# Matrices of group B beside the heads of group A, inverses on two engines beside the gates, and TensorE's order in the scan written by hand

## The chip, the cores and the metric

The kernel is one program on one core of a Trainium2 chip. The metric is its device time in microseconds (us). Engines: TensorE (PE in the profile; PEld is its weight load), VectorE (DVE), ScalarE (ACT), GpSimd (POOL) and SyncE (SP), whose one queue issues all of this kernel's DMA in order.

## The reference

One layer of a bidirectional recurrence backbone for 2048 latent and 128 context tokens, model width 1024: two head groups that read one input projection, an output projection, then a SwiGLU. Cut to what the change touches:

```python
def hgrn2_scan(q, k, v, g, s0):            # group A: 4 heads, two directions
    G = jnp.cumsum(g, axis=-2)
    q_dec, k_dec = q * jnp.exp(G), k * jnp.exp(-G)
    attn = jnp.where(causal, einsum(q_dec, k_dec), 0.0)
    ...                                     # S_t = diag(exp g_t) S_{t-1} + k_t v_t^T

def gated_delta_scan(q, k, v, beta, g, s0): # group B: 4 heads, two directions
    k_beta = k * beta[..., None]
    lower = jnp.where(strict, einsum(k_beta, k) * decay_mask, 0.0)
    sol = triangular_solve(lower + eye, concat([v * beta, k_beta * exp(G)]))
    u, w = sol[..., :dv], sol[..., dv:]
    attn = einsum(q, k) * decay_mask
    def step(s, inp):                       # one chunk after the other
        v_new = u_c - einsum(w_c, s)
        o_c = einsum(q_c, s) + einsum(attn_c, v_new)
        s = s * d_c + einsum(kt_c, v_new)

y = concat([o_a, o_b]) @ w_out              # after per-head norm and gate
x = x + g1 * y                              # then norm, SwiGLU, residual, final norm
```

## The kernel before, in words

Tokens are cut into 17 chunks of 128 (16 latent, one context, c = 16). Projections run as float32r triples (high by high, low by high, high by low part), in 5 pieces of 3 or 4 chunks. A plain float32 matmul has two records in the profile. The stages, in the order of the program:

- **Input norm and the convolved q, k, v of group B**, left in DRAM (`qkv_d`).
- **Heads of group A** (`for h in range(H)`): per head four projections and the chunked recurrence in both directions. Their matmuls write `pj`, `pa`, `pk`, `pu`, `po`.
- **The gate stage** (`sG`): eight gate projections (`gate_block`), and beside them the inverses of group B's triangular matrices, in three parts. `A1` makes a chunk's two matrices: k by k on PE into `pkk`, decays by a masked Exp, eight products on DVE, a sum on POOL, and a store. `A2` inverts all 32 x 32 diagonal blocks of a batch of chunks at once, in a chain of 60 dependent element-wise operations on one engine (tiles `pr`, `A`). `A3` puts a chunk's inverse together from the blocks by two levels of small matmuls (`pl`, `pn`), and stores it. There are five batches: four of four latent chunks, and the context chunk. `A2` runs on DVE for three batches and on POOL for two. `A1` has one buffer for the keys (`kTa`).
- **The scan of group B**, 16 iterations `i`: one chunk forward (c = i) and one backward (c = 15 - i). A scan step of one direction is six groups of four matmuls, `pkS`, `pv`, `pS`, `po`, `pa`, and `pqk` of the chunk that comes next. Between them lie the hops of the recurrence: `pkS`, then DVE makes `vn` (four operations, L929), `pv`, then ACT copies `vv` (L935), `pS`, then DVE makes the new state (L943). **Output steps** run beside it: `out_a` (norm, four transposes `ot`, gate, split in high and low), `out_b` (24 matmuls `py`, residual), `out_c` (norm and transposes `nt`, for five chunks). There are 34, one for each chunk and head group: the 17 of group A (part 0) can run at any time, the 17 of group B (part 1) only when both directions have passed the chunk, which for latent chunks is from i = 8 on. `first` and `todo` hold them. Before the loop eight part-0 steps are issued; the rest are spread so that part 0 is through by i = 7.
- **The SwiGLU** (`z`, `y`), in three sweeps.

Which instruction follows which on an engine is decided when the program is built, by the program's order, the priorities in it and a scheduler; each engine then runs its list in order. `tc.high_priority` moves a block ahead; `tc.issue_after` keeps a block behind an instruction.

Of the kernel before, what the change touches and what calls it, by code (L numbers as in the profile page):

```python
# [33 lines left out]
def hybrid_step(ctx: ExitStack, tc, x, vecs, ada1, ada2, bada, win, wgt, alog, dtb, sa, sb, wout, wg, wu, wd, normf,  # L34
# [106 lines left out]
    gq = pool(sK, "gq", right=True)  # L141
# [298 lines left out]

    with ExitStack() as sA:
        ap_ = pool(sA, "ap", 1)
        smask = ap_.tile([P, 512], F32, tag="smask", name="smask")
# [12 lines left out]
        for h in range(H):  # L456
# [3 lines left out]
            for i, (c0, n) in enumerate(PIECES):  # L460
# [4 lines left out]
                                               op1=ALU.mult)  # L465
            w = load_w(win[12 + h])
            for i, (c0, n) in enumerate(PIECES):
# [6 lines left out]
                nc.scalar.activation(out=vt[i], in_=pt[:, :n], func=AF.Copy, scale=0.5)  # L474
            for d in range(2):
# [7 lines left out]
                for i in order:  # L483
# [79 lines left out]
                    dma(out=oav[:, c0:c0 + n, h, :], in_=og)  # L563

    sp1.close()

    def bcast_G(t, d, c):
        dma(out=t.rearrange("p h t -> p (h t)"),
            in_=gr_d[d].rearrange("(c h) t -> c (h t)", h=H)[c:c + 1, :].broadcast_to([P, H * P]))
# [6 lines left out]
    psl = pool(s1b, "psl", 2, PSUM)  # L576
    psp = pool(s1b, "psp", 2, PSUM)


    with ExitStack() as sG:  # L580
        gp = pool(sG, "gp", right=True)
# [3 lines left out]

        def A1(c, b, j):

            kT = W([P, H, P], "kTa")
            dma(out=kT, in_=qkv_d[c, :, 0])
            pk = psp.tile([P, H, P], F32, tag="pre", name="pkk")  # L590
            for h in range(H):
                nc.tensor.matmul(out=pk[:, h], lhsT=kT[:, h], rhs=kT[:, h], start=True, stop=True)
            es = []
            for d in range(2):
                e = W([P, H, P], "e", 4)
                es.append(e)
                bcast_G(e, d, c)
                s = 1 if d == 0 else -1
                nc.gpsimd.affine_select(out=e, in_=e, pattern=[[0, H], [-s, P]], compare_op=ALU.is_gt, fill=1e30,
                                        base=0, channel_multiplier=s)  # L600
                for h in range(H):
                    nc.scalar.activation(out=e[:, h], in_=e[:, h], func=AF.Exp, scale=-1.0, bias=G[:, d, c, h:h + 1])
                for h in range(H):
                    nc.vector.scalar_tensor_tensor(out=e[:, h], in0=pk[:, h], scalar=nrho[:, d, c, h:h + 1],
                                                   in1=e[:, h], op0=ALU.mult, op1=ALU.mult)
            nc.gpsimd.tensor_tensor(out=es[0], in0=es[0], in1=es[1], op=ALU.add)
            dma(out=tri(b, j, [[P, P], [4 * BQ, H], [1, P]]), in_=es[0])

        def A2_load(b):
# [5 lines left out]
            B = W([P, 32, 32], "B")  # L615
# [10 lines left out]
        def A2(b, A, e=nc.vector):  # L626
# [4 lines left out]
            pr = W([P, 240], "pr")  # L631
# [6 lines left out]
            T = W([P, 32, 32], "B")  # L638
# [6 lines left out]
        XT = [W([P, 2, H, P], f"XT{i}") for i in range(2)]  # L645
        NS = [W([P, 2, H, 64], "NS")]
# [3 lines left out]
        def A3(c, b, j):  # L650
# [3 lines left out]
            xt = XT[n % 2]  # L654
            second = n >= NB[1] and n % 2 == 1

            dd = W([P, 2, 2, H, 32], "e", 4) if second else W([P, 2, 2, H, 32], "dd", 2)
            dma(out=dd.rearrange("p a d h s -> p (a d h) s"),
                in_=xi_d[b][j].rearrange("a d (h q) (i s) -> (q i) (a d h) s", q=4, s=32))
            L = W([P, H, P], "e", 4) if second else W([P, H, P], "L", 2)  # L660
            dma(out=L, in_=tri(b, j, [[P, P], [4 * BQ, H], [1, P]]))
            if second and len(NS) < 2:
                NS.append(W([P, 2, H, 64], "kTa"))
                nc.gpsimd.memset(NS[1], 0.0)
            na, s6 = (NS[int(second)][:, i] for i in range(2))
# [894 lines left out]
```

## Time and profile before

| | |
|---|---|
| median of 3 runs | 3353.89 us (3351.26 to 3354.86) |
| the profiled execution: time, span | 3358.57 us, 3356.9 us |
| PE busy, mean granted clock | 3121.5 us (93%), 0.964 of full speed |
| DVE, ACT, POOL busy | 2089.0, 1519.0, 1254.8 us |
| DMA, mean | 185 GB/s |

A busy PE is not a PE at its peak: a matmul's record is longer than its turn in a stream of them, and at half clock all of it takes twice as long. So stages are compared by the windows below, and matmuls are priced from the distance between the starts of two that follow each other closely.

### The profile page before, as it was taken

The numbers are of one execution on the slowest core, as the hardware profiler recorded it, in microseconds if no ns is written. First come the engines' busy times: TensorE is split into PE (matmuls) and PEld (weight loads), VectorE is DVE, ScalarE is ACT, GpSimd is POOL, SyncE is SP. The second block draws the span as 40 slices with busy tenths as digits, with TensorE's granted clock in tenths as the row PEclk, the third lists the DMA queues.
The fourth block names the chain that finished last, engine by engine and source line by source line (L and its number), as shares of the span: only waits on it lengthen the run. The fifth ranks groups of instructions, "written<-read, shape, count | busy, mean of one in ns | idle before, by whom it ended". The sixth has DMA issues, their size and how long they took to land. (4 is left out here: it accounts for less than half of the span.)

```text
span 3356.9 us, 51604 instructions
## 1 busy us (share of the span) xinstructions
PE 3121.5 (93%) x18550; PEld 2792.2 (83%) x18550; DVE 2089.0 (62%) x4016; ACT 1519.0 (45%) x3233; POOL 1254.8 (37%) x1228
## 2 busy tenths in 40 slices
PE   7899989999999799998897999999999999899998
PEld 4687779999998677877786888888899998799997
DVE  4667744474553764564666777778565677565667
ACT  6455435374464544663764555454422223422222
POOL 1100001021121337413566544554545553544446
PEclk8999999999999988999998999999999999999999
DMA  5235410111114667877784877898656766655564
GB/s 221 72 109 145 116 55 29 53 44 36 53 39 138 172 179 230 265 249 253 240 263 152 304 287 286 298 325 314 223 192 212 240 211 230 228 193 194 184 201 155
DMA packets 331009, 620.12 MB, mean 185 GB/s; under 512 B 77818, under 2 KB 177954, under 8 KB 324354
## 3 DMA queue, kind: packets, MB, share of 16 engines
q1 hardware_dynamic: 330754, 616.83, 56.0%
q8 instruction: 147, 2.41, 0.3%
q14 instruction: 108, 0.88, 0.1%
HBM read 435.22 MB, written 181.51 MB: 184 GB/s over the span
## 5 line engine op out<-in xcount | busy, mean ns | idle before, releaser
L257 PE MATMUL pj<-hh,wh 128*128 128x384 f32 (+2 forms) x1480 | 546.0, 369 | 12.9 <-DVE q L464 6.6
L257 PE MATMUL pj<-hl,wh 128*128 128x384 f32 (+2 forms) x1480 | 545.2, 368 | 0.3 <-POOL hl L231 0.3
L257 PE MATMUL pj<-hh,wl 128*128 128x384 f32 (+2 forms) x1480 | 545.3, 369 | 0.0
L257 PEld LDWEIGHTS pj<-hh,wh 128*128 128x128 f32 (+1 forms) x1480 | 280.4, 189 | 45.5 <-DVE q L464 6.8
L257 PEld LDWEIGHTS pj<-hl,wh 128*128 128x128 f32 (+1 forms) x1480 | 280.1, 189 | 29.9 <-issue 3.1
L257 PEld LDWEIGHTS pj<-hh,wl 128*128 128x128 f32 (+1 forms) x1480 | 280.1, 189 | 28.7 <-issue 3.3
L1476 POOL TENSOR_TENSOR u<-u,g 128x384 f32<-128x384 f32 (+1 forms) x132 | 136.3, 1033 | 292.7 <-DVE u L1217 242.8
L494 POOL TENSOR_SCALAR th<-th,nlbh,lbh 128x384 f32<-128x384 f32 (+1 forms) x40 | 60.5, 1513 | 405.8 <-ACT G L492 401.8
L1371 DVE TENSOR_TENSOR acc<-y,acc 128x512 f32<-128x512 f32 x192 | 131.7, 688 | 64.9 <-PE y L1367 58.0
L1209 PE MATMUL z<-x1h,wp 128*128 128x384 f32 (+1 forms) x528 | 142.8, 334 | 17.6 <-ACT wp L1067 14.2
L1067 ACT ACTIVATE wd<-wdr 128x512 fp32r<-128x512 f32 x146 | 90.0, 627 | 149.4 <-PE y L1367 95.4
L1367 PE MATMUL y<-wd,hid0h 128*128 128x512 f32 x432 | 136.4, 399 | 18.7 <-ACT hid0h L1067 10.0
L1464 ACT ACTIVATE g<-g 128x384 f32<-128x384 f32 (+1 forms) x132 | 66.7, 505 | 191.0 <-DVE g L1217 190.1
L1067 ACT ACTIVATE hid0h<-u 128x384 fp32r<-128x384 f32 (+3 forms) x113 | 53.3, 481 | 217.2 <-POOL u L1476 181.2
L1209 PE MATMUL z<-x6h,wp 128*128 128x384 f32 (+1 forms) x528 | 142.7, 333 | 7.2 <-ACT wp L1067 4.6
L246 DVE TENSOR_TENSOR wl<-raw,wh 128x512 fp32r<-128x512 f32 (+1 forms) x74 | 51.7, 698 | 153.6 <-ACT wh L245 153.5
L1371 DVE TENSOR_TENSOR sum<-y,sum 128x512 f32<-128x512 f32 x144 | 99.3, 690 | 75.8 <-PE y L1367 73.3
L1209 PE MATMUL z<-x4h,wp 128*128 128x384 f32 (+1 forms) x528 | 144.5, 331 | 1.3 <-DMA wp<-wpd 1.3
L1209 PE MATMUL z<-x7h,wp 128*128 128x384 f32 (+1 forms) x528 | 144.3, 332 | 1.0 <-DMA wp<-wpd 1.0
L1068 DVE TENSOR_TENSOR wd<-wdr,wd 128x512 fp32r<-128x512 f32 x146 | 111.9, 775 | 51.5 <-ACT wd L1067 50.6
L1209 PE MATMUL z<-x3h,wp 128*128 128x384 f32 (+1 forms) x528 | 142.6, 328 | 0.0
L1209 PE MATMUL z<-x2h,wp 128*128 128x384 f32 (+1 forms) x528 | 140.5, 328 | 1.4 <-DMA wp<-wpd 1.4
(414 smaller groups left out, 8850.6 us busy)
## 6 DMA issues: line engine op xcount, KB each, us to landing
wp<-wpd SPq DMA_DIRECT2D x308, 512.0 KB
wpd<-wp SPq DMA_DIRECT2D x154, 512.0 KB
ld<-qkvd SPq DMA_DIRECT2D x34, 1024.0 KB
wdr<-in_wd_dram SPq DMA_DIRECT2D x66, 512.0 KB
raw<-in_win_dram SPq DMA_DIRECT2D x72, 256.0 KB
e<-grd SPq DMA_DIRECT2D x68, 256.0 KB
at<-in_ada_dram SPq DMA_DIRECT2D x64, 256.0 KB
wr<-in_wg_dram SPq DMA_DIRECT2D x22, 512.0 KB
```

Of the source, the lines that this page charges most:

```text
L246: nc.vector.tensor_tensor(out=wl[:, ks], in0=raw, in1=wh[:, ks], op=ALU.subtract)
L257: nc.tensor.matmul(out=out, lhsT=a[:, k], rhs=b[:, k], start=t == 0, stop=t == 3 * KD - 1)
L494: nc.gpsimd.tensor_scalar(out=th, in0=th, scalar1=nlbh[:, col:col + 1], scalar2=lbh[:, col:col + 1], op0=ALU.mult, op1=ALU.add)
L1067: nc.scalar.activation(out=wh, in_=raw, func=AF.Copy)
L1068: (e or nc.vector).tensor_tensor(out=wl, in0=raw, in1=wh, op=ALU.subtract)
L1209: nc.tensor.matmul(out=z, lhsT=w_[:, k], rhs=x_[:, k, :N], start=t == 0, stop=t == 3 * HK - 1)
L1367: nc.tensor.matmul(out=py, lhsT=u_[:, j * P:j * P + P], rhs=v_, start=t == 0, stop=t == 2)
L1371: nc.vector.tensor_tensor(out=sums[i, j], in0=py, in1=sums[i, j], op=ALU.add)
L1464: nc.scalar.activation(out=g, in_=g, func=AF.Silu)
L1476: nc.gpsimd.tensor_tensor(out=us[i], in0=us[i], in1=gs[i], op=ALU.mult)
```

## The change

Three things are moved.

1. **Matrices beside the heads.** `A1` leaves the gate stage. Loads, decays and products of the 17 chunks are issued in small steps after the pieces of group A's projections (`beside`), with two buffers, in the space of a gate tile that is now given back earlier. Its `pkk` uses the PSUM tag `tr`, with two banks that `pk` and `ptv` of the heads use too.
2. **Inverses in two chains.** All `A2` are issued at the head of the gate stage, on DVE for batches 1, 2, 0 and on POOL for 3 and 4; then all `A3`, with three result tiles, two scratch tiles and four PSUM banks, then the gates.
3. **The scan's order on PE.** Inside `tc.manual_schedule(engines={PE})` PE keeps the order of the program. A scan step is a generator that yields after each group of matmuls; an output step is a list of pieces (three `py` matmuls, or four transposes), and the pieces are dealt out between the groups. An iteration takes two output steps throughout; the four parts of an output step lie in successive steps. Other engines are still ordered by the scheduler.

```diff
+        def A1(c, b, j, kT, es):
+            pk = ps1.tile([P, H, P], F32, tag="tr", name="pkk", bufs=2)
+            for h in range(H):
+                nc.tensor.matmul(out=pk[:, h], lhsT=kT[:, h], rhs=kT[:, h], start=True, stop=True)
...
+        chunk = [lambda: A1_decays(*held[0]), matrices]
+        steps = [load_next] * 2 + chunk * len(loads)
+        slots = [0, 5 * 4 * H]
+        def beside():
+            slots[0] += 1
+            while steps and len(steps) * (slots[1] - 8) > (slots[1] - 4 - slots[0]) * nsteps:
+                steps.pop(0)()
...
-        for t in range(5):
-            for j, c in enumerate(batches[order[t]]):
-                A1(c, order[t], j)
-            blocks.append(A2_load(order[t]))
-            if t:
-                chain(t - 1)
-            if t == 1:
-                levels(0)
-        chain(4)
-        for t in range(1, 5):
-            levels(t)
+        for b in (1, 3, 2, 4, 0):
+            with tc.high_priority(1000):
+                A2(b, A2_load(b), nc.gpsimd if b in (3, 4) else nc.vector)
+        for b in border:
+            for j, c in enumerate(batches[b]):
+                A3(c, b, j)
         for b in range(8):
             gate_block(b)
...
+    with tc.manual_schedule(engines={mybir.EngineType.PE}):
+        for _ in range(2):
+            for f in out_step():
+                f()
...
+        for i in range(NL):
+            cs = (i, NL - 1 - i)
+            gens = [scan(d, cs[d], pres[d]) for d in range(2)]
+            nxt = [scan_load(0, i + 1), scan_load(1, NL - 2 - i)] if i < NL - 1 else None
+            groups_ = [lambda g=g: next(g, None) for _ in range(5) for g in gens]
+            if nxt:
+                for d in range(2):
+                    groups_.append(lambda d=d: scan_pq(*nxt[d]))
...
+            for j, g in enumerate(groups_):
+                if j in (0, len(groups_) // 2):
+                    for f in fill:
+                        f()
+                    fill = out_step()
+                    left = len(groups_) // 2 if j == 0 else len(groups_) - j
...
+                g()
+                for _ in range(-(-len(fill) // left)):
+                    fill.pop(0)()
+                left -= 1
```

On PE, at the end of the gate stage (`pj` is a gate projection, `pl` and `pn` are `A3`, `ot` to `pv` the first output and scan steps). Before:

```order
L257 MATMUL pj<-hh_600,wl 128x384
L681 MATMUL pl_10216<-kTa,e 32x32 x16
...
L686 MATMUL pn_10332<-dd,NS 32x32 x4
L701 MATMUL pl_10347<-NS 64x64 x8
L675 MATMUL pl_10380<-e 32x32 x16
L820 MATMUL ot<-ident,o_12304 128x128
L905 MATMUL pqk<-ld 128x128 x4
L927 MATMUL pkS<-S_12783,ld 128x128
...
L681 MATMUL pl_10380<-kTa,e 32x32 x16
L686 MATMUL pn_10414<-e,kTa 32x32 x4
L933 MATMUL pv<-ld,XT 128x128 x4
```

In the change, the end of the last `A3` and what follows it:

```order
L736 MATMUL pl_10928<-XT_9256,L 64x64 x4
L726 MATMUL pn_10913<-dd,NS_9260 32x32 x4
L715 MATMUL pl_10961<-dd,L 32x32 x9
L741 MATMUL pl_10928<-NS_9260 64x64 x8
L721 MATMUL pl_10961<-NS_9259,dd 32x32 x16
L726 MATMUL pn_10995<-dd,NS_9259 32x32 x4
L736 MATMUL pl_11010<-XT_9257,L 64x64 x8
L726 MATMUL pn_10995<-dd,NS_9259 32x32 x4
L741 MATMUL pl_11010<-NS_9259 64x64 x8
L941 MATMUL pqk<-ld 128x128 x8
L961 MATMUL pkS<-S_12311,ld 128x128 x4
L880 MATMUL py<-woh,oh 128x512
```

Before, the last eight chunks of `A3` (of 17) stood between matmuls of the scan and of output steps, the very last after 240 `py`. Now nine chunks stand among the gates, the first after 267 matmuls of the gate projections that follow the last `po` of the heads, and eight stand alone after the last gate matmul, ahead of every scan matmul.

On PE in the scan, in an iteration past the middle, the first groups of both directions. Before (one direction; 20 `py` stand between `pkS` and `pv`, 16 of them left out here):

```order
L905 MATMUL pqk<-ld 128x128 x4
L847 MATMUL py<-woh,oh 128x512
L847 MATMUL py<-wol,oh 128x512
L847 MATMUL py<-woh,oh 128x512
L847 MATMUL py<-wol,oh 128x512
L927 MATMUL pkS<-S_15500,ld 128x128 x4
L847 MATMUL py<-woh,ol 128x512
...
L933 MATMUL pv<-ld,XT 128x128 x4
L947 MATMUL po<-S_15500,ld 128x128 x4
L820 MATMUL ot<-ident,ob 128x128 x4
L938 MATMUL pS<-vv,ld 128x128 x4
L954 MATMUL pa<-vv,e 128x128 x4
```

In the change:

```order
L961 MATMUL pkS<-S_15119,ld 128x128 x4
L906 MATMUL nt<-ident,xn 128x128 x4
...
L961 MATMUL pkS<-S_15132,ld 128x128 x4
...
L968 MATMUL pv<-ld,XT 128x128 x4
L849 MATMUL ot<-ident,ob 128x128 x4
L906 MATMUL nt<-ident,xn 128x128 x4
L968 MATMUL pv<-ld,XT 128x128 x4
...
L974 MATMUL pS<-vv,ld 128x128 x4
L880 MATMUL py<-woh,oh 128x512
...
L974 MATMUL pS<-vv,ld 128x128 x4
```

The two directions now run side by side, a half iteration's output step is dealt out in threes and sixes between their groups, and `po` and `pa` come behind both `pS`. The order of the SwiGLU's matmuls, from the first `z` on, and all matmuls ahead of the first `pkk` are the same in both programs.

## Rows read from the trace of the kernel before

**Rows 1.** Windows by stage: engine busy us (records), granted PE clock, DMA share, GB/s.
```profile
490.00:1038.00 548.00, 535.04 (x3247) 499.80 (x3248) 286.50 (x694) 279.97 (x439) 98.80 (x82) 0.99 0.14 43
1038.00:1298.00 260.00, 226.69 (x1805) 201.14 (x1805) 144.49 (x395) 126.82 (x256) 98.64 (x157) 0.93 0.64 175
1298.00:1316.00 18.00, 11.53 (x220) 10.60 (x214) 11.95 (x34) 14.32 (x44) 9.95 (x25) 0.58 0.89 265
1316.00:1525.00 209.00, 199.94 (x1801) 171.62 (x1799) 122.57 (x319) 129.64 (x388) 74.71 (x119) 0.95 0.80 263
1525.00:1610.00 85.00, 68.61 (x498) 64.70 (x497) 39.48 (x114) 34.97 (x99) 29.93 (x32) 0.93 0.75 255
1610.00:1803.00 193.00, 176.11 (x1061) 153.75 (x1061) 126.97 (x333) 123.17 (x348) 113.89 (x99) 0.94 0.72 231
1803.00:1835.00 32.00, 26.09 (x107) 19.33 (x105) 20.28 (x34) 11.12 (x37) 21.06 (x16) 0.84 0.48 164
1835.00:1848.00 13.00, 0.06 (x1) 0.00 (x0) 12.85 (x11) 5.65 (x12) 11.31 (x8) 0.71 0.37 120
1848.00:3357.00 1509.00, 1443.64 (x7722) 1334.56 (x7722) 1016.02 (x1677) 542.47 (x1039) 764.28 (x650) 0.98 0.69 238
```
**Rows 2.** PE groups, 1038 to 1316: count, busy us, mean ns, idle before and releaser.
```profile
L592 PE MATMUL pkk<-kTa 128*128 128x128 f32 x136 | 21.2, 305 | 30.8 <-DMA kTa<-qkvd 30.1 <-DVE pr L635 0.6
```
**Rows 3.** PE groups, 490 to 1038.
```profile
L521 PE MATMUL pk<-ident,e 128*128 128x128 f32 x136 | 26.9, 275 | 8.3 <-DVE e L516 8.3
```
**Rows 4.** PE timeline in the scan at full clock: start us, us, what.
```profile
1508.22 0.39 PE L847 MATMUL py<-woh,oh 128*128 128x512 f32 x1
...
1510.53 0.40 PE L847 MATMUL py<-wol,oh 128*128 128x512 f32 x1
...
1552.64 1.06 PE L954 MATMUL pa<-vv,e 128*128 128x128 f32 x8
1553.53 1.06 PE L905 MATMUL pqk<-ld 128*128 128x128 f32 x8
```
**Rows 5.** PE timeline, 1298 to 1316: small matmuls of A3 nearly alone.
```profile
1300.24 0.93 PE L696 MATMUL pl<-XT,e 64*64 64x64 f32 x16 [0.19 <-DVE XT L690]
...
1305.09 0.60 PE L686 MATMUL pn<-dd,NS 32*32 32x32 f32 x8
1308.85 1.57 PE L696 MATMUL pl<-XT,L 64*64 64x64 f32 x16 [3.16 <-DVE XT L690]
...
1313.38 1.57 PE L701 MATMUL pl<-NS 64*64 64x64 f32 x16 [2.40 <-ACT NS L698]
1314.88 1.35 PE L675 MATMUL pl<-e 32*32 32x32 f32 x32
```
**Rows 6.** Line L635 of A2: durations ns min/median/max, first and last start.
```profile
L635 DVE TENSOR_TENSOR pr<-A x90: 190/366/1373, 1095.8 to 1245.8; 128x30 f32<-128x30 f32 x6, 128x58 f32<-128x58 f32 x6, 128x84 f32<-128x84 f32 x6, 128x108 f32<-128x108 f32 x6
L635 POOL TENSOR_TENSOR pr<-A x60: 231/534/1376, 1246.3 to 1376.0; 128x30 f32<-128x30 f32 x2, 128x58 f32<-128x58 f32 x2, 128x84 f32<-128x84 f32 x2, 128x108 f32<-128x108 f32 x2
```
**Rows 7.** POOL groups, 1037 to 1320.
```profile
L606 POOL TENSOR_TENSOR e<-e 128x512 f32<-128x512 f32 x17 | 23.4, 1379 | 20.4 <-DVE e L604 16.9 <-DVE A L637 3.3
```
**Rows 8.** PE groups, 1316 to 1848.
```profile
L847 PE MATMUL py<-woh,oh 128*128 128x512 f32 x272 | 113.5, 417 | 4.6 <-ACT oh L822 4.0 <-DVE xt L855 0.5
...
L938 PE MATMUL pS<-vv,ld 128*128 128x128 f32 x272 | 42.7, 306 | 12.5 <-ACT vv L935 11.6 <-POOL A L637 0.8
```
**Rows 9.** PE groups, 1610 to 1803.
```profile
L927 PE MATMUL pkS<-S,ld 128*128 128x128 f32 x112 | 14.8, 275 | 0.0
```
**Rows 10.** Who PE waited for, 1316 to 1848: us in total, times, longest.
```profile
PE pS L938 <- ACT vv L935: 11.6, 13, 2.9
```
**Rows 11.** DVE, ACT and POOL groups, 1465 to 1835.
```profile
L929 DVE SCALAR_TENSOR_TENSOR ld<-pkS,nrg,ld 128x128 f32<-128x128 f32 x100 | 28.1, 342 | 8.8 <-PE pkS L927 7.0 <-DMA x<-in_x_dram 1.1
...
L935 ACT ACTIVATE vv<-pv 128x512 f32<-128x512 f32 x28 | 16.4, 584 | 23.5 <-PE pv L933 23.5
...
L908 POOL TENSOR_TENSOR ld<-ld,vbs 128x512 f32<-128x512 f32 x23 | 25.0, 1086 | 104.9 <-DMA ld<-qkvd 75.5 <-DVE ol L823 13.5 <-PE po L947 5.8
```

More of the change, by code (lines that the diff above doesn't have):

```diff
@@ L563, in hybrid_step @@
                     dma(out=oav[:, c0:c0 + n, h, :], in_=og)
+                    beside()
+        assert not steps
     sp1.close()
-    def bcast_G(t, d, c):
-        dma(out=t.rearrange("p h t -> p (h t)"),
-            in_=gr_d[d].rearrange("(c h) t -> c (h t)", h=H)[c:c + 1, :].broadcast_to([P, H * P]))
     def rep_h(m):
@@ L584, in W @@
             return gp.tile(shape, dt, tag=tag, name=tag, bufs=bufs)
[L586 to L607, printed above, removed]
         def A2_load(b):
@@ L909, in scan_pre, with scan_pq @@
                                     .to_broadcast([P, H, P]), op=ALU.mult)
+    def scan_pq(kT, qT, kn, vn, e, X):
+        pq = ps2.tile([P, H, P], F32, tag="pre", name="pqk", bufs=1)
+        for h in range(H):
+            nc.tensor.matmul(out=pq[:, h], lhsT=kT[:, h], rhs=qT[:, h], start=True, stop=True)
+        nc.vector.tensor_tensor(out=e, in0=pq, in1=e, op=ALU.mult)
     visited = set()
-    last = [None]
+    todo = []
     def scan(d, c, pre):
@@ L951, in scan @@
             dma(out=o_sb[d].rearrange("h k v -> k h v"), in_=Sn)
-        pa = sc_("pa")
-        for h in range(H):
-            last[0] = nc.tensor.matmul(out=pa[:, h], lhsT=at[:, h], rhs=vv[:, h], start=True, stop=True)
         second = c in visited
@@ L963, in scan @@
                 nc.scalar.activation(out=t[:, h], in_=po[:, h], func=AF.Copy, scale=eG[:, d, c, h:h + 1])
+        yield
+        pa = sc_("pa")
+        for h in range(H):
+            nc.tensor.matmul(out=pa[:, h], lhsT=at[:, h], rhs=vv[:, h], start=True, stop=True)
+        if lat:
             nc.vector.tensor_tensor(out=t, in0=pa, in1=t, op=ALU.add)
@@ L990, in scan_ctx @@
-    def scan_ctx():
-        ts = []
-        for d in range(2):
-            a = scan_load(d, NL)
-            scan_pre(d, NL, *a)
-            ts.append(scan(d, NL, a))
-            visited.discard(NL)
-        nc.gpsimd.tensor_tensor(out=ts[0], in0=ts[0], in1=ts[1], op=ALU.add)
-        return ts[0]
+        if not lat:
+            ctx_o.append(t)
+            if d:
+                nc.gpsimd.tensor_tensor(out=ctx_o[0], in0=ctx_o[0], in1=ctx_o[1], op=ALU.add)
+                todo.append((NL, 1, ctx_o[0]))
+            else:
+                visited.discard(NL)
+        elif not second:
+            dma(out=ob_d[c], in_=t)
+        else:
+            of = W([P, H, P], "or", 2)
+            dma(out=of, in_=ob_d[c])
+            nc.gpsimd.tensor_tensor(out=t, in0=t, in1=of, op=ALU.add)
+            todo.append((c, 1, t))
@@ L1002, in hybrid_step @@
     first = [(c, 0, None) for c in halves[0] + halves[1]]
-    todo = []
-    for _ in range(8):
-        out_step(first.pop(0))
     for d in range(2):
```

271 lines of the change are left out of this document (156 added, 115 removed).

## The prediction

> **What bounds the kernel now.** I read the page first, then windows cut at the stages. In the heads PE is busy 535.0 of 548 us at a granted clock of 0.99, and in the SwiGLU 1443.6 of 1509 us at 0.98: PE sets the time there, and the change leaves the SwiGLU's order alone [rows 1]. What can be won lies between 1038 and 1848 us. In the gate stage (1038 to 1298) PE is busy 226.7 of 260 us, and its groups say why: `pkk` waited 30.8 us, nearly all for the keys' DMA into a single buffer [rows 1, 2]. From 1298 to 1316 only the small matmuls of `A3` are there, and PE is at a clock of 0.58. Then comes the scan, 1316 to 1835, 519 us.
>
> To see how far the scan is from what its matmuls need, I price them by distance of starts at full clock. From the `py` at 1508.22 to the tenth after it at 1510.53 is 2.31 us, so 0.231 us each; a group of four float32 matmuls (eight records) follows the one before in 0.89 us, 0.111 a record [rows 4]. The scan has 816 `py` (three lines of 272) and six groups of 256 or 272 records each, 1600 in all [rows 8], and about 176 transposes at a record's price each: 188 + 178 + 20 = 386 us. Eight of the 17 chunks of `A3` lie in there too, by the order of the program. A chunk's small matmuls take 0.60 + 1.57 + 1.57 + two times 1.35 = 6.4 us at about half clock [rows 5], so some 3.2 at full clock, 26 us for eight. So PE needs 412 of the 519 us, 79%. The stretches differ. From 1525 to 1610 no output step is left that can run, the recurrence runs alone, and PE is busy 68.6 of 85 us. From 1610 to 1803, 14 steps of a direction (112 `pkS` records, eight a step) run with an output step beside each [rows 1, 9]. One costs six times 0.89, plus 24 times 0.231, plus 0.45 for transposes, 11.3 us; 14 make 159 of 193 us, 82%.
>
> No other engine is full: in that stretch DVE is busy 127 us, ACT 123, POOL 114 [rows 1], per iteration (two directions, 27.6 us) 18.1, 17.6 and 16.3 us. DMA moves 231 to 263 GB/s from 1316 to 1803, at a share of 0.72 to 0.80.
>
> **The change, part by part.**
>
> *Heads.* 17 chunks of `A1` add 136 records at 0.111, 15 us, on an engine that is full. Their work on ACT, DVE and POOL lies beside: these are busy 280, 287 and 99 of 548 us [rows 1]. `pkk` shares two PSUM banks with the transposes `pk`, which already wait 8.3 us for DVE in this stage [rows 3], so I add 2: **+17 us**. Bounds: 15 with no new wait; 50 if each of the 17 waits the 2 us that those four (one a head) do.
>
> *Gates.* From 1038 to 1316 are 278 us, with the gates, `A1` and nine chunks of `A3`. Out go the waits before `pkk`, 31, and its matmuls, 15; the 18 us alone at the end become a chunk and a half among gate matmuls, say 6 us, so 12 less [rows 1, 2]. The clock of 0.93 means that 14% of the stage ran at half speed, mostly where PE waited; I take 4 us back. That leaves 216 us. The first inverse is needed after 267 gate matmuls. The gates' own share is 216 less nine chunks at 3.2, 187 us, for 960 matmuls, 0.195 each: 52 us after the heads. A DVE chain alone is 60 operations at a median 0.366, a POOL chain 60 at 0.534 [rows 6], so 22 and 32 us, and with loads, a transposition and the splits of weights DVE's is ready well before. But the two have not yet run together: DVE's three end at 1246, POOL's begin at 1246.3 [rows 6]. The nearest sign of what they do to each other is that the longest DVE operation of the chain took 1373 ns, as long as POOL's sum of two matrices (mean 1379) that ran in the same stage [rows 6, 7]. If each operation waits out the other's, a pair takes 0.90 us and both chains 54; with some 8 us of loads ahead the first matmul of `A3` would stand on PE for 10 us, and all gate matmuls behind it. I take **6**, between 0 and 20. The stage: 222 for 278, **-56 us**.
>
> The Trainium skill, "SBUF — State Buffer", section "Who interferes with whom", says that a VectorE instruction with two SBUF inputs contends with a GpSimd instruction that reads SBUF. The trace's 1373 ns agrees; by that rule alone the term would be 10, not 6.
>
> *`A3` alone.* Eight chunks now stand behind the last gate matmul with nothing else for PE. Bounds: the matmuls at half clock, 6.4 us, or less where two chunks overlap and the clock holds (3.2); and the distance of two chunks at this same level now, 1300.24 to 1308.85, 8.6 us [rows 5]. ACT is shared with the first output steps as it is there, but there are three result tiles and four banks where there were two. I take 6: **+48 us**, between 26 and 69. The same eight leave the scan, which is counted next.
>
> *Scan.* An iteration is two steps of a direction and two output steps, 22.6 us by price. The hops: `vn` is four DVE operations of 342 ns, 1.4 us, `vv` one copy of 0.58 [rows 11]; between a `pkS` and its `pv` now lie six or nine `py`, the other direction's `pkS` and transposes, about 3.4 us, so that hop is covered unless its engine is late, and likewise `pv` to `pS` (2.5 us or more). The stretch without output steps is gone. In the first half I take PE at 86%: better than the 82% of 1610 to 1803, since part 0 has neither residual nor POOL work. With 45 `py` an iteration (the last four steps fall behind the loop) and 7 us for the context chunk that is 181 / 0.86 = 211. In the second half an iteration also moves, by the tiles in the code, two of each: `ld` 1024 KB, `XT`, `e`, `or`, `gt` 256 KB, `xt`, `x2` and its store 512 KB, in all 7.3 MB. At 82% PE gives 212 for eight; at 263 GB/s, the rate of the fullest long stretch [rows 1], the loads give 28 each, 223. I take 218. Behind the loop some 99 `py` at 0.231, 23 us, and waits, 32; ahead of it 4. The sum is 465 for 519, **-54 us**. Bounds: 386 / 0.92 = 420; and 386 / 0.76 = 508, below the worst long stretch.
>
> *Boundary to the SwiGLU.* 13 us with PE idle [rows 1]; its first weights are still loaded when the scan's tiles come free, so 0.
>
> Sum: 17 - 56 + 48 - 54 = -45 us. The profiled execution took 3358.6 (span 3356.9, the rest around it), which gives 3314; the median of the runs shown is 4.7 lower than that, so **3309**.
>
> **The rivals.**
>
> *A, the forecast:* about -45 (3285 to 3335).
>
> *B, the order covers all.* PE in the scan gets near its 96% busy of 1316 to 1525 without its half-clock stretches: 386 / 0.92 = 420 and `A3` at 4.5 a chunk: -45 - 45 - 12, some 3250. For it: the hops are covered two times over, and no engine is over 70% of an iteration. Against: two thirds of ACT, DVE and POOL each, in strict lists, make some operation late in every iteration.
>
> *C, the loads set the second half.* POOL already waits 75.5 us for `ld` in 1465 to 1835 [rows 11]. At 231 GB/s, the rate of 1610 to 1803, an iteration takes 32 us: +36 us, 3345. Against: that rate was not a limit, the share was 0.72.
>
> *D, the written order stalls, slower.* Today the scheduler may put `pqk`, `po` and 20 `py` wherever it found room; now a late hop stops everything behind it. The mechanism: `vv` waits in ACT's list behind eight Exps and eight squares of the output steps. PE waited 13 times for `vv`, at most 2.9 us [rows 10]. With four such hops an iteration (`vv` and the state, both directions), 64 in all, it is slower than before from 45 / 64 = 0.7 us a hop beyond my 82 to 86%; at 1.5 us each it would be +51, 3405.
>
> *E, a wash.* The tail of `A3` at 8.6 a chunk (+21) and the chains' wait at 20 (+14) leave -10: 3344.
>
> The bound of a change that can be told from none is about 0.2%, 7 us.
>
> **How the numbers follow.** A 0.42, B 0.20, C 0.15, D 0.14, E 0.09. Faster by over 0.2%: A, B, most of C and half of E, 0.78. Same: the rest of those two, 0.07. Slower: D and a little, 0.15. The range leaves out the lower part of B and D: 3245 to 3352. The likeliest case alone has 3285 to 3335.
>
> **What would show it.** Heads: longer by 15 to 20 us, `pkk` without waits over a few us in all. Gates: no wait for `kTa`; a wait of PE at the first `pl` for `XT` or `dd`, and longer medians in both chains, would show the two engines in each other's way. `A3` alone: a stretch of about 48 us with PE half idle and at a low clock, between the last `pj` and the first `pqk`. Scan: `pkS` of one direction every 26 us in the first half and 27 in the second, no stretch without `py`, clock above 0.97. Waits of PE at `pS` for `vv` far above 12 us would speak for D; PE waiting at `pv` or `pkS` for DMA, and a DMA share above 0.85, for C. I am wrong if the tail of `A3` is much longer than 48 us, or if the scan stays above 500.

## The result: 0.9% slower

The changed kernel took a median 3384.8 us (3383.2 to 3387.3), before 3354.4 beside it: ratio 1.0093, 95% interval 1.0076 to 1.0111. Forecast were 3309 and, at 0.78, a gain. The profiled execution has a span of 3384.2 for 3356.9, so 27.3 us are to be found. First windows by stage of the changed kernel, columns as in [rows 1]:

```profile
488.00:1074.00 586.00, 555.13 (x3376) 513.53 (x3376) 328.82 (x830) 316.26 (x572) 140.46 (x133) 0.98 0.25 71
1074.00:1312.00 238.00, 214.95 (x1872) 191.38 (x1870) 82.97 (x224) 76.37 (x120) 88.92 (x178) 0.94 0.50 127
1312.00:1403.00 91.00, 60.31 (x901) 54.56 (x901) 53.67 (x148) 46.48 (x129) 23.68 (x43) 0.52 0.75 245
1403.00:1619.00 216.00, 199.95 (x1283) 174.41 (x1282) 117.67 (x316) 119.14 (x364) 49.15 (x52) 0.97 0.69 231
1619.00:1835.00 216.00, 185.84 (x1190) 163.93 (x1189) 143.69 (x375) 124.47 (x380) 116.32 (x103) 0.95 0.69 230
1835.00:1867.00 32.00, 25.10 (x105) 19.44 (x104) 21.06 (x30) 8.41 (x27) 26.51 (x20) 0.89 0.59 200
1867.00:1881.00 14.00, 0.72 (x3) 0.30 (x2) 13.43 (x10) 5.87 (x12) 12.79 (x9) 0.65 0.46 150
1881.00:3384.00 1503.00, 1443.52 (x7722) 1336.07 (x7721) 1012.98 (x1678) 542.91 (x1039) 764.62 (x650) 0.98 0.70 239
```

The cuts are the last `po` of the heads, the last gate matmul, the first `pkS` (1318 before, 1403 after), the middle of the scan, the last `py` and the first `z`. In these cuts, with the forecast's terms (222 + 48 + 4 for the two in the middle):

| stretch | before | forecast | measured | miss |
|---|---|---|---|---|
| heads, change | | +17 | +36 | 19 |
| last head to last gate | 260 | 222 | 238 | 16 |
| last gate to first `pkS` | 20 | 52 | 91 | 39 |
| first `pkS` to last `py` | 517 | 461 | 464 | 3 |
| last `py` to the end | 1522 | 1522 | 1517 | -5 |

The misses add to 72, and -45 + 72 is the measured +27. The scan came out at the length forecast; the stages ahead of it did not. The stretch of 91 us is the one to look at: PE at a granted clock of 0.52 and busy 60 of 91, DMA at 245 GB/s.

Then PE's groups in the heads (488 to 1075), beside [rows 3]:

```profile
L618 PE MATMUL po<-T,e 128*128 128x128 f32 x256 | 52.4, 287 | 11.9 <-DVE T L616 11.3
L605 PE MATMUL po<-vt,am 128*128 128x128 f32 x272 | 52.4, 277 | 6.9 <-ACT og L627 6.9
...
L590 PE MATMUL pk<-ident,e 128*128 128x128 f32 x136 | 26.7, 275 | 0.0
L476 PE MATMUL pkk<-kTa 128*128 128x128 f32 x136 | 19.1, 275 | 0.0
```

`pkk` itself waits for nothing, and the 8.3 us that `pk` waited in [rows 3] are gone. But the `po` matmuls of the recurrence, which waited for nobody before, now wait 19 us for VectorE's `T` and ScalarE's `og`.

Whom PE waited for from 1074 to 1403, the four largest (us in total, times, longest):

```profile
PE pl L736 <- DVE XT L730: 12.6, 6, 7.4
PE pl L715 <- issue: 8.8, 1, 8.8
PE pl L715 <- DMA dd<-xid: 7.9, 1, 7.9
PE pl L741 <- ACT NS L738: 5.4, 3, 2.6
```

The 30 us for the keys of [rows 2] are gone; the 8.8 and 7.9 are the first `A3` of batches 1 and 2 (at 1142.6 and 1241.9), whose inverses were late. The longest wait of the tail, in VectorE's timeline and then PE's:

```profile
1355.62 0.18 DVE L681 TENSOR_TENSOR A<-A,pr 48x30 f32<-48x30 f32 x1
1355.83 1.03 DVE L683 COPY B<-A 48x1024 f32<-48x1024 f32 x1
1356.89 1.22 DVE L730 COPY XT<-pl 32x128 f32<-32x128 f32 x4
```
```profile
1357.62 1.57 PE L736 MATMUL pl<-XT,L 64*64 64x64 f32 x16 [7.40 <-DVE XT L730]
```

The context batch's inverse, 60 operations on VectorE that began at 1297, stands in that engine's list ahead of `A3`'s copies to `XT`, and PE waits for the copy. The end of the tail on PE:

```profile
1395.80 1.57 PE L741 MATMUL pl<-NS 64*64 64x64 f32 x16 [0.62 <-ACT NS L738]
1398.48 2.05 PE L941 MATMUL pqk<-ld 128*128 128x128 f32 x8 [1.11 <-DVE XT L744]
1401.37 2.07 PE L941 MATMUL pqk<-ld 128*128 128x128 f32 x8 [0.84 <-DVE e L942]
```

`A3` fills 85 of the 91 us, with about eight chunks (seven of them whole), 10.7 us each; PE waits 28 of the 85 us for copies. The scan's first matmuls, behind it, wait hardly at all.

### The profile page after: what moved, and what is told of

It reads as the page before. It is cut to its first block, busy times and chain, and to the rows that moved or that the text cites. A ratio compares the mean times of both kernels' runs of the same rounds, so it can differ in the third digit from the quotient of the medians.

```text
span 3384.2 us, 51481 instructions
## 1 busy us (share of the span) xinstructions
PE 3117.7 (92%) x18550; PEld 2789.9 (82%) x18550; DVE 2080.9 (61%) x4016; ACT 1490.9 (44%) x3215; POOL 1254.6 (37%) x1229
## 5 line engine op out<-in xcount | busy, mean ns | idle before, releaser
L1284 PE MATMUL z<-x5h,wp 128*128 128x384 f32 (+1 forms) x528 | 141.2, 331 | 0.3 <-DMA wp<-wpd 0.3
```

What stands on the lines that cost most here:

```text
L1284: nc.tensor.matmul(out=z, lhsT=w_[:, k], rhs=x_[:, k, :N], start=t == 0, stop=t == 3 * HK - 1)
```

## The experiments

Each is given with its ratio to before and 95% interval; `x` numbers are labels. Before itself had medians of 3350 to 3355 in the six groups. The heads of the changed kernel ended at 1072.7 to 1074.4 in the eight profiles that have its heads (last `po`), but those of x10, x11, x12 and x14, one and the same code, anywhere from 1068.5 to 1075.6 (last `pu`), so a difference of a few us between two profiles is not read.

**The heads.** x7 takes before and does part one alone:

```diff
+ steps = [load_next] * 2 + [lambda: A1_decays(*held[0]), matrices] * 17    # beside() as in the change
- for j, c in enumerate(batches[order[t]]):
-     A1(c, order[t], j)
  blocks.append(A2_load(order[t]))
```

> Before with part one alone: A1 of all chunks beside the heads, A2, A3, their order and the scan as before. Theory: heads 36 us longer, as in the changed kernel, and the gate stage shorter by pkk's 31 us of waits and 15 us of matmuls, 46: 3354 - 10 = 3344, between 3334 and 3354. Rival (the chains, still one after the other, set when A3 can stand among the gates, so what the gates save comes back as chunks in the scan): 3360 to 3385.

Measured: 3358.8, 1.0018 (1.0006 to 1.0029): slower, if by little, and outside the theory's range. Heads +36 as expected; the last gate matmul stands at 1319.2, the last `py` at 1842.3, for 1297.7 and 1835.1. From the heads' end to the last `py` that is 28 us less, not 46, so the price in the heads exceeds the gain. Where the other 18 us went was not tested; the rival, that they come back as chunks in the scan, is open. x15 and x16 take work out of `A1` in the changed kernel:

```diff
- for d in range(2): for h in range(H): stt(e[:, h], pk[:, h], nrho, e[:, h])    # 8 products
+ stt(es[0][:, 0], pk[:, H - 1], nrho[:, 0, c, 0:1], es[0][:, 0])                # x15: one
- for h in range(H): activation(e[:, h], Exp, bias=G[:, d, c, h:h + 1])          # 4 a direction
+ activation(e[:, 0], Exp, bias=G[:, d, c, 0:1])                                 # x16: one
```

> The changed kernel with one of the eight products of A1 on VectorE per chunk left out of none but the first (seven of eight are not computed), and zeros stored as the matrices, so the results are not the reference's. TensorE, ScalarE and the order are as in the changed kernel. Theory: of the 36 us that the heads grew, 20 are pkk's matmuls and their share of the clock, 16 waits of PE for VectorE's T and ScalarE's og, which stand in their lists behind A1's products and Exps; without the products the wait for T goes back to nothing: last po at 1062, between 1058 and 1066, for 1074. Rival (the waits come from the loads' traffic or from pkk's bank): 1072 or later.

> The changed kernel with two of the eight Exps of A1 on ScalarE per chunk (six are left out), and zeros stored as the matrices. Theory: the wait of po for og goes, 7 us, that for T stays: last po at 1067, between 1064 and 1070. Rival (og waits for something else): 1073 or later.

Measured: x15 3367.0, 1.0042 (1.0027 to 1.0057); x16 3376.0, 1.0062 (1.0030 to 1.0094). The last `po` ended at 1060.8 in x15 and 1062.7 in x16, for 1074.2. The same groups, x15 (488 to 1061), then x16 (to 1063):

```profile
L605 PE MATMUL po<-vt,am 128*128 128x128 f32 x272 | 51.9, 275 | 0.0
L618 PE MATMUL po<-T,e 128*128 128x128 f32 x256 | 50.6, 279 | 2.4 <-DVE T L616 1.8
...
L590 PE MATMUL pk<-ident,e 128*128 128x128 f32 x136 | 26.6, 274 | 8.0 <-DVE e L585 8.0
```
```profile
L608 PE MATMUL po<-vt,am 128*128 128x128 f32 x272 | 52.9, 279 | 0.0
L621 PE MATMUL po<-T,e 128*128 128x128 f32 x256 | 51.7, 284 | 6.1 <-DVE T L619 5.7
...
L593 PE MATMUL pk<-ident,e 128*128 128x128 f32 x136 | 27.0, 277 | 6.5 <-DVE e L588 6.5
```

With the products gone the wait before these `po` falls from 11.9 to 2.4, and either edit frees `og`; `pk` waits again, 8.0 and 6.5. x15 did what the theory said; x16 beat its 1067, since the wait for `T` fell there too. So `A1`'s products alone cost 13 of the 36 us, and its Exps alone 11; the two overlap and do not add. Both engines are under 60% busy in the stage.

**The inverses one after the other.** In the changed kernel VectorE's and GpSimd's chains alternate: 1088 to 1118, 1128 to 1183, 1193 to 1220, 1239 to 1287, 1297 to 1356. x4 gives each chain's masks and transposing copy to its own engine:

```diff
- nc.vector.tensor_copy(out=A[pb:np_], in_=B[pb:np_] transposed); nc.gpsimd.affine_select(A)
+ e.tensor_copy(out=A[pb:np_], in_=B[pb:np_] transposed)
+ e.affine_select(A) if e is nc.gpsimd else e.tensor_tensor(out=A, in0=A, in1=low, op=mult)
```

> The changed kernel with each inverse's preparation on its own engine: masks and the transposing copy of the VectorE batches on VectorE, those of the GpSimd batches on GpSimd, so that no chain waits for the other engine's chain (one buffer of L less to make room). Theory: batch 3 starts beside batch 1 and the context batch is done before the last gate; the tail of A3 (same order of chunks on PE, eight or so alone) shrinks from 85 to about 60, and the 17 us of PE's waits for dd and issue in the gate stage go: 3384 - 35 = 3350, between 3335 and 3365. It also shows whether the two engines slow each other: if yes, VectorE's operations of the chain (median 0.33 us) come near GpSimd's 0.53. Rival: the tail is set by half clock, the one SP queue and hops: 3375 to 3390.

Measured: 3387.5, 1.0102 (1.0088 to 1.0117), no better than the changed kernel and in the rival's range, and the chains alternated as before. SyncE's timeline of x4 shows why:

```profile
1075.81 1.98 SPq L663 DMA_DIRECT2D A<-ld  x2
1077.84 1.71 SPq L663 DMA_DIRECT2D B<-ld  x1
...
1112.98 0.61 SPq L689 DMA_DIRECT2D xid<-A  x1
1113.64 0.60 SPq L663 DMA_DIRECT2D B<-ld  x1
1114.33 5.92 SPq L689 DMA_DIRECT2D xid<-B  x2
```

The second `B` load (batch 3's) stands in SP's one list behind the store of batch 1's inverse, which waits for that chain to end; GpSimd waited 39.3 us for it. So the masks alone, my first theory, were not it. x5 puts the loads ahead as well, and there the chains do run together:

```diff
- for b in (1, 3, 2, 4, 0): A2(b, A2_load(b, e), e)
+ As = {b: A2_load(b, eng(b)) for b in (1, 3)}
+ for b, n in ((1, 2), (3, 4), (2, 0), (4, None), (0, None)):
+     A2(b, As[b], eng(b))
+     if n is not None: As[n] = A2_load(n, eng(n))
```

> As the run side by side, and each batch's matrices are loaded (and masked) ahead of the stores of the chain before: loads of batches 1 and 3, then chain 1, loads of 2, chain 3, loads of 4, chain 2, loads of 0, chains 4 and 0. In the run side by side the chains still followed each other, since the loads of B and A stood in SP's queue behind the stores of the running chain. Now the builder puts the first chunk of A3 16 gate matmuls earlier and 15 of 17 chunks ahead of the last gate matmul. Theory (the tail is chunks left over because the chains ran one after the other): gates and A3 take about 254 to 270 us as with early inverses, no tail beyond 20 us, heads as in the changed kernel: 3384 - 50 = 3334, between 3318 and 3350. Rival one (a chunk's hops set its 10 us also here, and hold up the gates): 3365 or more. Rival two (VectorE and GpSimd in each other's way): VectorE's operations of the chain rise from a median 0.35 to 0.45 or more, both chains of a pair end together, time 3345 to 3365.

Measured: 3370.6, 1.0056 (1.0042 to 1.0070). 15 chunks of `A3` stood among the gates, and the first `pkS` came at 1389.9, for 1403.2. But the gate stage was 271 us at PE busy 241. The chains' groups in VectorE's list, first alone (the changed kernel, 1088 to 1118), then beside GpSimd's (x5, 1085 to 1124), then GpSimd's of x5 (1090 to 1152):

```profile
L679 DVE TENSOR_TENSOR pr<-A 128x30 f32<-128x30 f32 (+14 forms) x30 | 10.0, 332 | 2.4 <-POOL A L665 1.4
L681 DVE TENSOR_TENSOR A<-A,pr 128x30 f32<-128x30 f32 (+14 forms) x30 | 10.0, 332 | 1.0
```
```profile
L684 DVE TENSOR_TENSOR A<-A,pr 128x30 f32<-128x30 f32 (+14 forms) x30 | 17.2, 574 | 1.0
L682 DVE TENSOR_TENSOR pr<-A 128x30 f32<-128x30 f32 (+14 forms) x30 | 16.8, 560 | 1.0
```
```profile
L684 POOL TENSOR_TENSOR A<-A,pr 128x30 f32<-128x30 f32 (+14 forms) x30 | 16.5, 550 | 2.4
L682 POOL TENSOR_TENSOR pr<-A 128x30 f32<-128x30 f32 (+14 forms) x30 | 15.9, 529 | 2.3
```

Beside GpSimd's chain VectorE's operations take 567 ns for 332; GpSimd's take 540, as alone in the changed kernel (522). In the middle of x5's chains, on GpSimd and then VectorE:

```profile
1096.81 0.54 POOL L684 TENSOR_TENSOR A<-A,pr 128x168 f32<-128x168 f32 x1
```
```profile
1097.01 0.59 DVE L682 TENSOR_TENSOR pr<-A 128x228 f32<-128x228 f32 x1
```

VectorE's operation starts beside GpSimd's and ends 0.25 us after it, and so do its neighbours. The Trainium skill, "SBUF — State Buffer", section "Who interferes with whom", calls the port pair that the two engines share an exclusive lock. The trace agrees for one side: VectorE waits out GpSimd's operation, but GpSimd hardly waits for VectorE's, and a pair takes some 0.60 us where 0.33 and 0.52 one after the other would take 0.85. The theory's 3334 fell: the tail was 46 us for at most 20, and PE was idle for 30 us of the gate stage. Rival two had VectorE's slowdown right; the time fell in rival one's range.

x12 and x13 take one of the two engines away. Both compute early inverses in the heads (as x3 below), batch 1's (x12) or those of 1 and 2 (x13), and run the rest of them on VectorE alone (x12) or on GpSimd alone (x13); x10 is as x12, but with a chain on each.

```diff
- EARLY = (1, 2, 3)                                    # x3
+ EARLY = (1,)                                         # x10, x12; (1, 2) in x13
- eng = lambda b: nc.gpsimd if b in (3, 4) else nc.vector
+ eng = lambda b: nc.vector                            # x12; nc.gpsimd in x13; x10 as it was
+ for b, n in ((2, 4), (3, 0), (4, None), (0, None)):  # x12; loads of 2 and 3 ahead
```

> The changed kernel with the inverse of batch 1 alone on GpSimd in the heads (one buffer for A1's tiles there, as with early inverses), and in the gate stage batches 2 (VectorE) and 3 (GpSimd) loaded first and run together, then 0 and 4. All 17 chunks stand among the gates. Theory: heads end at 1074 + 8 = 1082 (early inverses, three of them: 1097); gates 254 to 262; then 27 of loads, scan and boundary 499 - 27: 3351 - 15 = 3336 to 3344. Rival (the one buffer, not the chains, costs the 23 us in the heads): 3351 to 3360.

> As the run with one early inverse, but the four inverses left for the gate stage all run on VectorE, one after the other, and none on GpSimd. In the run with one early inverse a VectorE chain beside GpSimd's took a mean 0.52 us an operation where it takes 0.33 alone, and gates and A3 took 275 us; with early inverses, where one short chain of each engine was left, 254. Theory (the two chains hold each other up, and A3's copies behind them): VectorE's operations fall to 0.33 to 0.36, no wait of PE behind them over 5 us, gates and A3 254 to 260, heads as with one early inverse: 3359 - 17 = 3342, between 3334 and 3350. Rival (what holds A3 up is its own copies in VectorE's list behind any chain): 3355 to 3370.

> Inverses of batches 1 and 2 on GpSimd in the heads, and the other three on GpSimd in the gate stage, none on VectorE. Theory: no VectorE chain beside GpSimd's, so A3's copies on VectorE run free; heads 10 us longer than with one early inverse, gates and A3 254 to 260: 3359 - 8 = 3350, between 3340 and 3356. Rival (GpSimd's own chain delays A3's copies to NS, which stand in the same list): gates 270 and more, 3360 to 3370.

Measured: x10 3358.9, 1.0026 (1.0012 to 1.0039); x12 3361.9, 1.0031 (1.0019 to 1.0042); x13 3350.0, 1.0002 (0.9991 to 1.0013). The gate stages, x12 and x13:

```profile
1084.00:1358.00 274.00, 251.39 (x2752) 221.62 (x2750) 130.69 (x407) 94.02 (x166) 28.92 (x75) 0.94 0.48 132
```
```profile
1082.00:1346.00 264.00, 250.40 (x2752) 221.36 (x2750) 54.13 (x150) 92.94 (x166) 130.15 (x268) 0.95 0.48 131
```

x10's and x12's theories fell. x13's time held, though its gate stage took 264 and not 254 to 260. In x12 the operations are back at 339 ns, as expected, yet the stage is no shorter than x10's 275: PE waits 14.5 us once for a `dd`. But the edit did not do all that was meant: the scheduler wove the inverses of batches 2 and 3 together on VectorE (1099 to 1147), so batch 2's came no earlier than beside GpSimd's chain (x10, 1090 to 1134). Taking the other engine away does not help by itself; that a late inverse sets the stage, on whichever engine, fits x10, x12 and x13 but was not tested alone. The heads ended 3 to 10 us after the changed kernel's (last `pu` 1068.5 to 1075.6 for 1065.6), not 23, so the one buffer is not the cost in x3's heads that x10's rival made it; but what the heads gave back, the gate stage took.

**The tail of `A3`.** x3 computes the inverses of batches 1 to 3 on GpSimd in the heads, with one buffer for `A1`'s tiles to make room:

```diff
+ def chain(b):                      # three rounds of 30 at each beside(), on nc.gpsimd
+     A = A2_load(b, V, 1, nc.gpsimd); yield
+     yield from A2(b, A, V, 1, nc.gpsimd)
- for b in (1, 3, 2, 4, 0): A2(...)
+ for b in (4, 0): A2(...)
```

> The changed kernel with the inverses of three batches (1, 2, 3) computed on GpSimd during the heads, three rounds a slot, so that the first twelve chunks of A3 can start with the gates; A1's tiles in the heads have one buffer instead of two to make room. All 17 chunks then stand among gate matmuls. Theory (the tail is long since the inverses come late): the 324 us from the last head to the scan become 215 busy + 8 chunks at 3.4 + some waits = 250 to 270, time 3384 - 60 = 3325, between 3310 and 3340. Rival one (a chunk's own hops set its 10.6 us, also beside gates): 3360 or more. Rival two (GpSimd's 180 operations hold up the heads, by its list or by slowing VectorE): heads 20 to 40 us longer, 3345 to 3365.

Measured: 3354.8, 1.0004 (0.9994 to 1.0015), 30 us under the changed kernel, level with before. Its windows, gate stage and then the last gate to the first `pkS`, and the DMA view of the second:

```profile
1097.00:1351.00 254.00, 248.88 (x2750) 219.87 (x2749) 73.32 (x212) 93.45 (x165) 61.89 (x140) 0.97 0.48 132
1351.00:1378.00 27.00, 6.01 (x27) 4.96 (x26) 11.73 (x28) 20.00 (x56) 5.73 (x7) 0.56 1.02 344
```
```profile
DMA packets 4787, 9.29 MB, mean 344 GB/s; under 512 B 410, under 2 KB 2890, under 8 KB 4210
```

The 3325 fell. All 17 chunks and the gates took 254 us, so a chunk's hops hide well among gates (rival one falls). Rival two holds for the heads, which ended 23 us later than the changed kernel's, with PE idle for 47 us where it was 31. And there is a stretch that the forecast did not have: with no `A3` left, PE does 6 us of work in 27, while the loads of the first output and scan steps fill DMA. SyncE issues the first `ld` 6 us after the last gate matmul, behind the loads of the output steps; PE waits 11.7 us for an output step's `o` on ScalarE and 7.5 for the first `pqk` product. x8 and x9 price the chunks: the last seven are not computed (the tile is stored as it is), with the written order (x8) and with the scan of before (x9).

```diff
+ if n >= 10:
+     dma(out=xt_d[c], in_=xt)
+     return
```

> The changed kernel without the work of A3 for the last seven chunks (it stores the tile as it is; their results are left out), the rest as it is: ten chunks among the gates, then the scan in the written order. Theory (with the written order nothing lies beside those chunks, so each costs all its 8 to 10 us; but the scan's loads need some 27 us after the gate stage's buffers come free, as with early inverses, and that stays): the 86 us from the last gate to the first pqk become 27, time 3385 - 59 = 3326, between 3316 and 3340. Rival (the loads, started behind A3's, or the late context chain set the 85 us): 3355 or more.

> The same seven chunks' A3 left out of the run with the scan of before. Theory: in the scan of before the builder puts these chunks between output steps and scan, so they cost 4 to 5 us each, 30 in all: 3374 - 30 = 3344, between 3334 and 3354; so the written order by itself, without A3 in its way, is worth 3344 - 3326 = 18 us, and the changed kernel loses that and more by what the order makes A3 cost. Rival (the forecast's reading: a chunk costs the same either way and the order is worth nothing or 28): equal to the run above, or 28 and more slower.

Measured: x8 3330.5, 0.9935 (0.9915 to 0.9955); x9 3323.4, 0.9913 (0.9895 to 0.9931). Against the changed kernel and x1 (below) the seven chunks are worth 0.0158 of before in both, 53 us, 7.6 each. x8's theory held (3326); for x9 I had expected 4 to 5 a chunk, and that fell. x8, last gate to the last `py`:

```profile
1311.00:1347.00 36.00, 11.32 (x118) 9.66 (x117) 30.80 (x83) 19.59 (x56) 8.16 (x9) 0.55 0.98 354
1347.00:1812.00 465.00, 408.98 (x2575) 357.00 (x2574) 287.00 (x726) 263.76 (x799) 197.35 (x180) 0.97 0.74 239
```

36 us stay without the chunks, 9 more than in x3. The end of an `A3` that began ahead of the last gate takes the first of them (to 1320), and then PE waits 18.2 us for a `pqk` product on VectorE, which stands behind the context batch's inverse. The decays that it needs and the product, on ScalarE and VectorE:

```profile
1336.59 1.28 ACT L936 ACTIVATE e<-e,nG 128x128 f32<-128x128 f32 x4
```
```profile
1343.81 1.03 DVE L683 COPY B<-A 48x1024 f32<-48x1024 f32 x1
1344.76 0.67 DVE L945 TENSOR_TENSOR e<-pqk,e 128x512 f32<-128x512 f32 x1
```

So some 11 us of the wait are for the decays, whose loads came late, and 7 for the inverse. In the changed kernel this time lies under `A3`: `pqk` there waits 1.1 and 0.8 us (above). The 36 us are a floor under the tail and not a part of its 91. x11 has x10's code, with the first steps' scan loads issued ahead of the output weights:

```diff
+ pres = [scan_load(0, 0), scan_load(1, NL - 1)]
+ for d in range(2): S[d] = W([P, H, P], f"S{d}", 2); dma(out=S[d], in_=sb[d])
  for k in range(H): load_wout(k)
```

> The run with one early inverse, and the first two steps' scan loads and the states are issued ahead of the output weights and the gates of the output steps. Theory: of the 27 us between the last gate and the first pkS, in which DMA is full (344 GB/s), those loads (3.5 MB) need 10, so 8 to 12 us less: 3326 to 3336, faster than before and than the changed kernel. Rival (the loads start only when the gate stage's buffers come free, and the output steps that then come late are needed as filling): no change within 5 us.

Measured: 3363.2, 1.0035 (1.0020 to 1.0049), the first `pkS` at 1377.7 for 1378.7: no gain, as its rival said. But SyncE's list hardly changed: the first `ld` was issued at 1359.0, behind the loads of `wor`, `o` and `gt` as in x10 (1358.5). So the edit did not put these loads first, and whether room or order sets the 27 us stays open.

**The written order.** x1 is the changed kernel with the scan of before, x2 before with the written scan alone, x6 is x5 and x14 is x12 with the scan of before. The edit is one and the same, all code from `out_a1` (`out_a` before) to the end of the loop, which has one buffer more for `x2` and `ob` in the written order; its core:

```diff
- with tc.manual_schedule(engines={mybir.EngineType.PE}):
-     for j, g in enumerate(groups_):
-         g(); fill.pop(0)()
+ for d, c in ((0, i), (1, NL - 1 - i)):
+     o = scan(d, c, pres[d])
+ for _ in range(n): out_step(...)
```

> The changed kernel with the scan of before (its code from the output steps to the end of the loop), so parts one and two of the change alone. Theory: the stages add up, heads +36, gates -39, and the 85 us in which A3 stood alone are not all spared, but its last chunks fall into the scan again, which costs the 519 us of before with 7 chunks in it: 3354 + 36 - 39 + 3 chunks alone (25) = 3376, between 3350 and 3380. Rival: part three is what lost the time (its fixed order puts A3 ahead of the scan), so without it the kernel is faster than before: 3320 to 3345.

> Before with the written scan order alone (part three), heads and gate stage as before. Theory: the scan's order is worth some 50 us by itself, and the 8 to 10 chunks of A3 that are left after the gates cost 3 to 9 us each: 3354 - 50 - 5 + (24 to 80 less the 26 that they took in the scan before) = 3325 to 3350, most likely 3335. Rival: the 50 us are only the eight chunks of A3 that left the scan, and the order itself brings nothing: 3350 to 3360.

> The run with loads ahead, but with the scan of before. With nearly all of A3 out of the scan in both, their difference is the worth of the written order alone. Theory, from the first runs (with both parts one and two, the written order gained 8 us between the last gate and the end of the scan, and lost 25 without them): it is worth little, within 12 us either way of the run with loads ahead. Rival (the forecast's): it is worth the 54 us less the 26 of A3, so this run is 20 to 35 us slower than the run with loads ahead.

> The run with one early inverse and the rest on VectorE, with the scan of before. No A3 is left in either scan. Theory (the written order is worth nothing where no A3 is in its way: the two runs without seven chunks differed by 7 us in favour of the scan of before): within 10 us of the run with the written order, on the faster side if at all. Rival (written order worth 28): 20 us or more slower.

| chunks begun behind the last gate | written order | scan of before | written order is worth |
|---|---|---|---|
| 9 (gate stage of before) | x2 1.0076 | before | -25 us |
| 7 (changed gate stage) | 1.0093 | x1 1.0071 | -7 |
| 2 | x5 1.0056 | x6 1.0070 | +5 |
| none, seven left out | x8 0.9935 | x9 0.9913 | -7 |
| none, all among the gates | x12 1.0031 | x14 1.0069 | +13 |

x1's theory held (3374), x2's fell (3335 expected, 3377 measured), x6's held, and x14's fell by a little (13 us for at most 10). x2 lost 19 of its 25 us between the last gate and the first `pkS`, 39 us for 20. The windows of x9 and x14 beside x8's above and x12's 487 us (1358 to 1845), last gate to first `pkS`, and on to the last `py`:

```profile
1310.00:1335.00 25.00, 17.81 (x144) 14.35 (x143) 21.91 (x67) 15.64 (x47) 4.45 (x3) 0.66 0.97 328
1335.00:1807.00 472.00, 416.39 (x2551) 361.31 (x2549) 286.84 (x741) 280.16 (x817) 202.83 (x186) 0.96 0.75 246
```
```profile
1353.00:1374.00 21.00, 10.72 (x40) 8.15 (x39) 12.15 (x30) 17.66 (x51) 2.93 (x4) 0.67 0.99 353
1374.00:1851.00 477.00, 420.23 (x2558) 365.50 (x2556) 281.99 (x724) 279.08 (x814) 200.71 (x185) 0.95 0.73 239
```

Once `A3` is out, the scan of before takes 472 to 477 us and the written one 462 to 465. At its start the written order loses again: its list holds next to nothing ahead of the first `pqk`, and PE does 6 to 11 us of work up to the first `pkS`, for 11 to 18 with the scan of before. Of the table's differences only the -25 and the +13 stand clear of their intervals. They follow the chunks in front of the scan only in the main: x8 and x9, with none begun there, have -7, with the late context inverse still in both.

What the chunks cost in the scan of before is seen in x1, last gate to first `pkS`, and on to the last `py`:

```profile
1312.00:1426.00 114.00, 99.19 (x1093) 81.72 (x1093) 77.68 (x213) 68.23 (x222) 23.66 (x43) 0.76 0.77 248
1426.00:1860.00 434.00, 381.93 (x2385) 334.60 (x2383) 252.70 (x655) 236.37 (x680) 189.88 (x174) 0.95 0.70 232
```

That is 548 us with PE busy for 481, where x9 without the chunks has 497 and 434: 47 of the 51 us are PE's own time, at a granted clock of 0.76 in the first stretch. In the written order 51 of 54 are (changed kernel and x8).

## Why the prediction was wrong

- **Heads, +17.** The matmuls' part was right, the waits' was not: +36, of which PE's busy time is 20 (535 to 555) and its idle time 16 (15 to 31). I had given 2 us to waits and looked for them at `pkk` and `pk`. They came at `po`, whose `T` and `og` queue behind `A1`'s products and Exps (x15, x16). With the products gone PE is busy 549 us, 14 more than before, near my 15. My upper bound of 50 held.
- **Gates, 222.** 238. The keys' waits went as said. The 6 us for two chains in each other's way had no object, since the chains never ran together; their late results cost 17 us of PE's waits at the first `A3` of two batches. When they do run together VectorE slows by 1.7 (x5). I had let each engine wait out the other, 0.90 us a pair; it was 0.60, since only VectorE waits.
- **`A3` alone, 48, and the start of the scan, 4.** This is the step that failed: 91 us for 52. I took 6 us a chunk, at most 8.6, from two chunks that had stood alone before. It was 10.7: 85 us for eight, with PE at half clock and 28 us of waits for copies, the longest behind the context batch's inverse. And I took the scan to start at once behind the tail. Under it lies a floor that I did not have: without the seven chunks only 53 us come back (x8), since 36 us of first loads, of the last chunk's end and of the late context inverse stay; with no `A3` at all 27 do (x3). In before 20 us passed between the last gate and the first `pkS`, and two chunks lay in them; I had called that stretch `A3`'s.
- **Scan, 465.** Measured 464 from the first `pkS`, for the 461 of the forecast, but not for the reason given; that the number fits is in part luck. I took 26 of the gain of 54 for the chunks that leave and the rest for the order. The scan of before without the chunks takes 472 (x9) for 517, so their leaving brings 45, and the order 7. I had priced them at full clock there, 3.2 each; they cost 7.6, nearly all of it PE's time (x1, x9), so what the scan gains by their leaving the tail takes back. The order by itself was worth between +13 and -25 us.
- **Boundary and SwiGLU, 0.** -5; not explained. From run to run the SwiGLU takes 1497 to 1509 us, whatever is changed ahead of it.
- **The rivals.** None was it. E came nearest, with the tail at a higher price; D gave a slower kernel, but by hops that stall, and they did not (the scan is 3 us off).

What stays open: what sets the 27 us before the scan, room or the order of the loads, and why the clock falls around the chunks in x1 although PE is busy 99 of 114 us there. The gate stage takes 254 us in x3 and 264 to 275 in x10, x12 and x13 mostly by waits: PE is idle 5 us in x3 and 14 to 23 in the others. No version that does all the work beat before: x3 and x13 are level with it and about 1% under the changed kernel.

## What to carry to other kernels

When work is moved out of one stage into another, price it in both by leaving it out, not by its matmuls: here it cost 7.6 us a chunk on either side, and the gain and the loss were one sum counted with two prices. What a stretch of work takes in the trace is not yet what its removal brings: the tail took 85 us, and without seven of its eight chunks 53 came back. Ask of each stage boundary what its first loads wait for; a tail of small work may hide the time in which the next stage's tiles come in. Engines that are 55% busy still delay a recurrence when a block of eight operations stands ahead of its one short step.

## What the runs showed of the hardware

- VectorE's operations on two SBUF inputs took a mean 567 ns beside GpSimd's of the same kind and 332 without; GpSimd's took 540 and 522. The loss was nearly all on one side (x5 and the changed kernel).
- DMA moved 344 GB/s at a share of 1.02 over 27 us in x3 and 353 at 0.99 in x14, far above the 263 that the forecast took for the fullest long stretch [rows 1].
- PE was at a granted clock of 0.52 over the 91 us of small matmuls and waits, near half speed for nearly the whole stretch; in x1, with output steps beside the chunks, it was 0.76, and in x3, with the chunks among gate matmuls, the gate stage had 0.97.
